# First stage of a hybrid decoder layer: q, k, v of two neighbouring heads and one gate, in wider weight runs, with a new order of heads and groups

## The chip, the cores and the metric

The kernel runs on one core of a Trainium2 chip. A core has a matrix engine (TensorE, PE in the profile), three engines for element-wise work (VectorE or DVE, ScalarE or ACT, GpSimd or POOL), a queue engine (SyncE, SP) that issues most transfers, and 16 DMA engines that move data between HBM and the on-chip memory. The metric is device time in microseconds (us), lower is better.

## The reference

One inference step of one layer, for a prompt of 1024 tokens and for 8 sequences of one new token each, in float32 with width 2048. What matters here, shortened:

```python
def mixer_layer(x, c, ...):
    mod = silu(c) @ w_ada + b_ada                       # w_ada 2048 x 6144
    shift, scale, gate = split(mod, 3)
    h = rmsnorm(x, norm_g) * (1 + scale) + shift
    z = h @ w_in                                        # w_in 2048 x 8208
    b_a, c_a, h_a, g_a, qkv, g_b, beta_logit, alpha_logit = split(z)
    # A: 8 groups of 128 channels
    y_a = b_a * causal_conv3(c_a * h_a) * silu(g_a)
    # B: 8 heads of 128
    q, k, v = split(silu(causal_conv4(qkv)))
    q, k = l2norm(q), l2norm(k)
    o, s = gated_delta_rule(q, k, v, g, beta, s0)       # chunked, one state per head
    o = rmsnorm(o, o_norm_g) * silu(g_b)
    y = concatenate([y_a, o]) @ w_out                   # 2048 x 2048
    return x + gate * y, ...
```

A final RMSNorm follows. The convolution states and the delta-rule states are outputs too.

## The kernel before, in words

**Layout.** Activations are kept transposed, channels on the 128 partitions and tokens along the free axis. The tokens go in two halves: 512 prompt tokens first, then 512 prompt tokens with the 8 samples. In each half `w_in` is taken in columns of 128 channels, each the k, q, v or gate of one head (`h(i, part)`, parts 0 to 3) or the C, h, gate or B of one group (`a(i, part)`, where part 0 is the two columns C and h). A `product` of a column sums 16 tiles of 128 rows in a PSUM bank. For precision, weights and activations are split in a high and a low fp32r part, and three passes (`hh·whi`, `hl·whi`, `hh·wlo`) are summed, so a product in the first half is 48 matmuls of 512 tokens.

**Weights.** `Stream` loads weights in tiles `raw` of 256 KB through SP's queue (six buffers), in the order in which they will be used. For each, ScalarE makes `whi`, and GpSimd or VectorE makes `wlo` (three buffers of each). SP's queue works in order: a load that waits for a free `raw` buffer holds up what is issued behind it.

**First stage (the ramp).** The conditioning product `silu(c) @ w_ada` needs 64 tiles `wat` of 512 KB, in runs of 1 KB (steps of two row tiles) or 2 KB (steps of four). It goes in six steps (`steps`), each giving shift and scale for 2 or 4 row tiles of `h`: `matvec` sums on TensorE, `spread` evicts the sums, transposes them and makes `s1` and `sh`, and `make_h` makes the row tiles `hh` and `hl`. Beside it, products of seven columns are accumulated in seven PSUM banks `pss`, row tile by row tile as `h` comes (`first_products`): C, h and gate of group 2, and k, q, v and gate of head 2 (`FIRSTS = (2, 2)`). Six of these columns have "pair" tiles: two row tiles of two columns, loaded by two issues of 128 KB with runs of 512 B (`add_pair`). The seventh has tiles of its own (`RONE`). Dummy matmuls (`busy`, 214 at the most) run at the very start. While TensorE would wait for `wat` tiles, `fill` gives it products.

**After it.** The logits of the decay gates follow (`logits_part`, on tiles `wlt`), then the remaining columns in the order that `order(half)` writes out by hand, then the output projection. The heads' delta rule runs beside the products: `gdn_prep`, `gdn_invert` (a triangular solve on VectorE with round trips through memory: `ub`, `tb`, `xd`, `yc`, issued from ScalarE's queue) and `gdn_apply`, one `chain` per head in the order `HEADS` = 2, 1, 3, 4, 7, 5, 0, 6. `conv_silu` evicts a k, q or v bank to `zr` on ScalarE and then does the convolution on VectorE, a tanh on ScalarE and a product on VectorE.

**The planner.** All engines work in order, and the order of the instructions is made when the program is built: `_Order` keeps a clock for each engine, with estimated costs (in `_Tensor.mm` for matmuls, in `_transfer` for transfers). Side work is written as generators that yield what they wait for; between matmuls, `pump` runs those steps whose inputs are ready by these clocks. So a changed cost or order moves side steps to other places in the stream. The price of a matmul of the fp32r kind was

```python
            if rhs.dtype == F32R:
                cost = max(n / 2250.0, 0.05) + 0.004
```

whatever stands before it. Line 370 in the profile is the call in `mm`, line 321 that of the other engines' operations; both are helpers, so groups are told apart by tile names.

Of the kernel before, what the change touches and what calls it, by code (L numbers as in the profile page):

```python
# [16 lines left out]
P = 128  # L17
# [345 lines left out]
class _Tensor:  # L363


    def __init__(self, od, pe):
        self.od, self.pe = od, pe

    def mm(self, out, lhsT, rhs, cost=None, **kw):
        r = self.pe.matmul(out, lhsT, rhs, **kw)  # L370
        if cost is None:
            n = _size(rhs)
            if rhs.dtype == F32R:
                cost = max(n / 2250.0, 0.05) + 0.004
            elif kw.get("is_transpose"):
                cost = 0.109
            else:
                cost = max(4 * n / 2400.0, 0.21) + 0.006
        self.od.put("P", [lhsT, rhs], [out], cost)
        return r  # L380


def _trunk(ctx, tc, nc, xT, w_in, w_ada, w_out, pack, consts, vecs, csq, ssm, yT, cap, cqp, ssp, cas, cqs, sss):
# [18 lines left out]
    def mm_tile():  # L402
        return ps_mm.tile([P, 512], F32, tag="mm", name="mm")
# [169 lines left out]
    class Stream:  # L573
# [9 lines left out]
                src = w[kq * 512:(kq + 1) * 512, col:col + P].rearrange("(k p) n -> p k n", p=P)  # L583
                self.todo.append(((col, kq), [(0, 4, src)]))

        def add_pair(self, w, cols, kp):

            self.todo.append(((cols, kp), [
                (2 * i, 2 * i + 2, w[kp * 256:(kp + 1) * 256, c:c + P].rearrange("(k p) n -> p k n", p=P))
                for i, c in enumerate(cols)]))  # L590

        def landed(self):

# [9 lines left out]
        def ahead(self, most=SPL):  # L603

            while True:
                if self.loaded < min(self.split + (4 if self.eager else RAW), len(self.todo)):
                    raw = wp.tile([P, 4, P], F32, tag="raw", name="raw", bufs=RAW)
                    for a, b, src in self.todo[self.loaded][1]:
                        SY.dma_start(raw[:, a:b, :], src)
                    self.raws.append(raw)  # L610
                    self.loaded += 1
                elif most and self.split < min(self.freed + SPL, self.loaded) and (
                        self.eager or self.split < self.used + 2 or self.landed()):
                    whi = wp.tile([P, 4, P], F32R, tag="whi", name="whi", bufs=SPL)
                    wlo = wp.tile([P, 4, P], F32R, tag="wlo", name="wlo", bufs=SPL)
                    split_w(self.raws[self.split], whi, wlo)
                    self.raws[self.split] = None
                    self.done.append((whi, wlo))
                    self.split += 1
                    most -= 1  # L620
                else:
                    return
# [151 lines left out]
        yield  # L774
        return th

    def conv_silu(half, t, pss, blocks, out, ready, zr=None):

        own = zr is None
        if own:  # L780
            hold("zr", 2)
            zr = tp.tile([P, WH + 3], F32, tag="zr", name="zr")
        for ps, (a, b) in zip(pss, blocks):
            S.activation(zr[:, 3 + a:3 + b], ps[:, :b - a], AF.Copy)
        if half == 0:
            G.memset(zr[:, 0:3], 0.0)
        else:
            G.tensor_copy(zr[:, 0:3], halo[:, t, :])

        def rest():  # L790
            yield [zr[:]]
            if half:
                G.tensor_copy(zs[:, t, :], zr[:, 3 + HT:3 + WH])
            G.tensor_copy(halo[:, t, :], zr[:, HT:HT + 3])
            w = [pkv("wq", t * 4 + j, 1) for j in range(4)]
            V.tensor_scalar(out, zr[:, 0:HT], w[0], None, ALU.mult)
            for j in range(1, 4):
                V.scalar_tensor_tensor(out, zr[:, j:j + HT], w[j], out, ALU.mult, ALU.add)
            if own:
                held["zr"] -= 1  # L800
            yield
            th = yield from tanh_half(out, HT)
            V.scalar_tensor_tensor(out, th[:, :HT], 1.0, out, ALU.add, ALU.mult)
            held["tm"] -= 1
            ready.append(out)
        od.spawn(rest())
# [450 lines left out]
    nca = cp.tile([P, 8, 2, NS], F32, name="nca")  # L1257
    sta = pkv("sa").rearrange("p (g j b) -> p g j b", j=2, b=NS)

    def group_a(half, g, blocks, y, pch=None):  # L1260
        n = WH if half else HT
        pc = pch[0] if pch else product(w_in, 1024 + g * P, range(4), hs, blocks)
        hold("ca", 1)
        c_ = tp.tile([P, WH], F32, tag="ca", name="c_", bufs=1)
        for ps, (a, b) in zip(pc, blocks):
            S.activation(c_[:, a:b], ps[:, :b - a], AF.Copy)
        phh = pch[1] if pch else product(w_in, 2048 + g * P, range(4), hs, blocks)
        hold("zr", 2)
        u = tp.tile([P, WH + 3], F32, tag="zr", name="ua")
        for ps, (a, b) in zip(phh, blocks):  # L1270
# [22 lines left out]
            held["zr"] -= 1  # L1293
        od.spawn(conv())
        yield
        pg = pch[2] if pch else product(w_in, 3072 + g * P, range(4), hs, blocks)
        hold("ca", 1)
        gc = tp.tile([P, WH], F32, tag="ca", name="gc", bufs=1)
        for ps, (a, b) in zip(pg, blocks):
# [17 lines left out]
            V.tensor_tensor(y[:, a:b], y[:, a:b], ps[:, :b - a], ALU.mult)  # L1317
        yield

    def head_tile(half, h, part, t, blocks, pss=None, zr=None):  # L1320

        if part < 3:
            c0 = 4096 + (1, 0, 2)[part] * 1024 + h * P
        else:
            c0 = 7168 + h * P
        if pss is None:
            pss = product(w_in, c0, range(4), hs, blocks)
        if part < 3:
            out = t["v"][:, :HT] if part == 2 else t["kq"][:, part, :]
            conv_silu(half, (1, 0, 2)[part] * 8 + h, pss, blocks, out, t["ready"], zr)  # L1330
            return
        n = WH if half else HT
        gb = t["gb"]
        for ps, (a, b) in zip(pss, blocks):
            S.activation(gb[:, a:b], ps[:, :b - a], AF.Copy)

        def silu():
            yield [gb[:]]
            th = yield from tanh_half(gb[:, :n], n)
            V.scalar_tensor_tensor(gb[:, :n], th[:, :n], 1.0, gb[:, :n], ALU.add, ALU.mult)  # L1340
            held["tm"] -= 1
            t["ready"].append(gb)
            if half:
                yield
                G.tensor_copy(gbs[:, h, :], t["gb"][:, HT:WH])
                sampled.append(h)
        od.spawn(silu())
# [7 lines left out]
    def order(half):  # L1355


        def h(i, *parts):
            return [("h", i, part) for part in parts or range(4)]

        def a(i, *parts):
            return [("a", i, part) for part in parts]
        if half == 0:
            r = a(2, 2) + h(1) + a(1, 0) + h(3) + a(1, 1) + h(4) + a(1, 2) + h(7, 0) + a(3, 0) + h(7, 1) + a(3, 1)
            r += h(7, 2) + a(3, 2) + h(7, 3) + h(5) + a(4, 0) + h(0, 0) + a(4, 1) + h(0, 1) + a(5, 0) + h(0, 2) + h(6)
            r += a(4, 2) + h(0, 3) + a(0, 0) + a(5, 1, 2) + a(0, 1) + a(6, 0) + a(0, 2)
            return r + a(6, 1) + a(7, 0) + a(6, 2) + a(7, 1, 2)
        r = h(2) + a(2, 0) + h(1) + a(0, 0) + h(3) + a(0, 1) + a(2, 1, 2) + a(0, 2) + a(1, 0) + h(4)
        r += h(7, 0) + a(1, 1, 2) + h(7, 1) + a(3, 0) + h(7, 2) + h(5) + h(7, 3) + a(3, 1, 2)
        r += h(0, 0) + a(4, 0) + h(0, 1) + a(4, 1, 2) + h(0, 2) + h(6) + h(0, 3)  # L1370
        return r + a(5, 0, 1, 2) + a(7, 0) + a(6, 0) + a(7, 1) + a(6, 1, 2) + a(7, 2)

    FIRSTS = (2, 2)
    HEADS = [i for kind, i, part in order(1) if (kind, part) == ("h", 0)]
    LASTG = order(1)[-1][1]

    HCOLS, ACOLS = (5120, 4096, 6144, 7168), (1024, 2048, 3072, 0)
    ADA = 9

    ra, rh = (tuple(c + i * P for c in cols) for cols, i in zip((ACOLS, HCOLS), FIRSTS))  # L1380
    RCOLS, RONE = (ra[:2], rh[:2], rh[2:]), ra[2]
    for kp in range(NK // 2):
        for c in RCOLS:
            ws.add_pair(w_in, c, kp)
# [51 lines left out]
    with ExitStack() as pools:  # L1436
# [17 lines left out]
        def first_products(f, nf):  # L1454

            for i in range(3):
# [2 lines left out]
                whi, wlo = rw[i]  # L1459
                for j in range(2):  # L1460
                    for k in range(f, f + nf):
                        jj = 2 * j + k % 2
                        passes(pss[2 * i + j], whi[:, jj, :], wlo[:, jj, :], *hs[k], 0, HT, k == 0, k == NK - 1)
                        yield
                if i == 2 and (f + nf) % 4 == 0:
# [81 lines left out]
        for step, (f, nf) in enumerate(steps):  # L1547
# [11 lines left out]
            for _ in spreading:  # L1559
                pass  # L1560
            if step == 0:
                pss = [mm_tile(), mm_tile(), mm_tile(), tp_tile(), ch_tile(), o_tile(), ch_tile()]
            for k in range(f, f + nf):
                if k % 4 == 0:
                    hs += h_quad()
# [9 lines left out]
                pass  # L1575
        S.activation(wl[:, :, 0:16], lr, AF.Copy)
        V.tensor_tensor(wl[:, :, 16:32], lr, wl[:, :, 0:16].bitcast(F32), ALU.subtract)
        ramp = [[p] for p in pss]
        od.rings = 1.0
        od.spawn(ws.run())  # L1580

# [83 lines left out]
    for half in range(2):  # L1665
# [3 lines left out]
        with ExitStack() as pools:  # L1669
# [6 lines left out]

            def chain(h, half, queue, done, gp):

                while len(queue) <= h or len(queue[h]["ready"]) < 2 or recd[half] < h - 1:
                    yield 0.2  # L1680
                t = queue[h]
                yield [t["kq"][:], MARGIN]
                cx = yield from gdn_prep(half, HEADS[h], gp, t)
                yield from gdn_invert(half, h, gp, t["kq"], cx)
                yield from gdn_apply(half, h, HEADS[h], gp, done, cx, t["kq"], t["gb"])

# [8 lines left out]
            def head(i, parts, pss=None):  # L1695
                for part in parts:
# [8 lines left out]
                    if part == 2:  # L1705
                        t["v"] = od.pin(yp.tile([P, WH], F32, tag="y", name="v"))
                    zr = yp.tile([P, WH], F32, tag="y", name="zr0") if pss and part < 3 else None
                    head_tile(half, i, part, t, blocks, [pss[part]] if pss else None, zr)

            groups = {}  # L1710
            if half == 0:
                g0 = FIRSTS[0]
                ys[g0] = new_y()
                groups[g0] = group_a(0, g0, blocks, ys[g0], (ramp[0], ramp[1], ramp[6]))
                next(groups[g0])
                next(groups[g0])
                head(FIRSTS[1], range(4), [r[0] for r in ramp[2:6]])
                od.spawn(conditions())
            pl = [mm_tile() for _ in blocks]
            for k in range(NK):  # L1720
# [210 lines left out]
```

## Time and profile before

| | us |
|---|---|
| median of 3 runs | 2144.99 (2144.23 to 2147.16) |
| profiled execution, its own time | 2149.42 |
| its span, first to last instruction | 2147.6 |
| TensorE busy in the span | 2108.6 (98%) |
| VectorE busy | 1252.4 (58%) |
| ScalarE busy | 832.6 (39%) |
| GpSimd busy | 849.0 (40%) |

Two rows of the page show the first stage: it cuts the span in 40 slices of 53.7 us, and gives the busy share of the DMA engines in tenths and what they moved. In the first two slices the DMA engines are at nine tenths, with 317 and 331 GB/s; from the fourth on they are mostly at half. The granted clock of TensorE is 0.993 over the span.

### The profile page before, as it was taken

The numbers are of one execution on the slowest core, as the hardware profiler recorded it, in microseconds if no ns is written. First come the engines' busy times: TensorE is split into PE (matmuls) and PEld (weight loads), VectorE is DVE, ScalarE is ACT, GpSimd is POOL, SyncE is SP. The second block draws the span as 40 slices with busy tenths as digits, with TensorE's granted clock in tenths as the row PEclk, the third lists the DMA queues.
The fourth block names the chain that finished last, engine by engine and source line by source line (L and its number), as shares of the span: only waits on it lengthen the run. The fifth ranks groups of instructions, "written<-read, shape, count | busy, mean of one in ns | idle before, by whom it ended". The sixth has DMA issues, their size and how long they took to land.

```text
span 2147.6 us, 40476 instructions
## 1 busy us (share of the span) xinstructions
PE 2108.6 (98%) x15045; PEld 1851.5 (86%) x15045; DVE 1252.4 (58%) x3635; ACT 832.6 (39%) x1885; POOL 849.0 (40%) x819
## 2 busy tenths in 40 slices
PE   8999999999999999999999999999999999999997
PEld 6468777777887887878889999999999999999997
DVE  3346776756867745287124767646576486435544
ACT  3234333434443333343233334243443333335554
POOL 1223333434344444423434343444443433445544
PEclk8999999999999999999999999999999999999998
DMA  9974765897454456955444564568664446968766
GB/s 317 331 231 83 159 147 145 137 159 135 113 114 96 88 106 84 82 180 181 142 104 105 125 120 108 121 107 110 112 91 91 90 100 100 91 92 239 228 210 203
DMA packets 466598, 299.66 MB, mean 140 GB/s; under 512 B 37600, under 2 KB 429536, under 8 KB 466400
## 3 DMA queue, kind: packets, MB, share of 16 engines
q1 hardware_dynamic: 442608, 284.26, 61.7%
q10 hardware_dynamic: 23792, 12.81, 2.5%
q8 instruction: 118, 1.93, 0.4%
q14 instruction: 80, 0.66, 0.1%
HBM read 277.06 MB, written 19.94 MB: 138 GB/s over the span
## 4 chain that ended last, share of the span: by engine, by line
PE 52%; DVE 2%; DMA 1%; POOL 0%; issue 0%; ACT 0%; POOLq 0%; ACTq 0%; DVEq 0%
PE mm L370 48%; PE cht L370 2%; PE tpt L370 1%; DVE xb L321 1%; PE ot L370 1%; DVE ob L321 0%; DMA tb<-ub 0%; DVE kq L321 0%; POOL wlo L321 0%; DMA ub<-dU 0%; POOL res L321 0%; DVE sl L321 0%; DVE y L321 0%; DVE wlo L321 0%; DMA xr<-in_xT 0%
## 5 line engine op out<-in xcount | busy, mean ns | idle before, releaser
L321 POOL TENSOR_TENSOR wlo<-raw,whi 128x512 fp32r<-128x512 f32 x547 | 731.4, 1338 | 1204.6 <-ACT whi L321 1026.9
L370 PE MATMUL mm<-hh,whi 128*128 128x264 f32 (+1 forms) x3008 | 969.2, 322 | 5.4 <-ACT hh L321 1.9
L370 PE MATMUL mm<-hl,whi 128*128 128x264 f32 (+1 forms) x3008 | 968.1, 322 | 5.2 <-DVE hl L321 5.0
L370 PE MATMUL mm<-hh,wlo 128*128 128x264 f32 (+1 forms) x3008 | 968.7, 322 | 0.6 <-POOL wlo L321 0.6
L321 ACT ACTIVATE whi<-raw 128x512 fp32r<-128x512 f32 x672 | 421.2, 629 | 686.3 <-PE mm L370 473.5
L370 PEld LDWEIGHTS mm<-hh,whi 128*128 128x128 f32 x3008 | 566.9, 188 | 54.0 <-issue 7.7
L370 PEld LDWEIGHTS mm<-hl,whi 128*128 128x128 f32 x3008 | 567.0, 188 | 50.0 <-DVE hl L321 7.4
L370 PEld LDWEIGHTS mm<-hh,wlo 128*128 128x128 f32 x3008 | 567.0, 188 | 41.4 <-issue 1.7
L370 PE MATMUL mm<-yhi,wlo 128*128 128x512 f32 (+2 forms) x768 | 246.1, 320 | 3.9 <-POOL wlo L321 3.2
L370 PE MATMUL mm<-ylo,whi 128*128 128x512 f32 (+2 forms) x768 | 246.3, 321 | 0.0
L370 PE MATMUL mm<-yhi,whi 128*128 128x512 f32 (+2 forms) x768 | 245.7, 320 | 0.0
L321 DVE TENSOR_TENSOR ob<-tb,xb 128x62 f32<-128x62 f32 (+30 forms) x992 | 200.7, 242 | 3.6 <-DMA tb<-ub 3.6
L321 DVE TENSOR_TENSOR xb<-xb,ob 128x62 f32<-128x62 f32 (+30 forms) x992 | 202.6, 244 | 0.0
L370 PEld LDWEIGHTS mm<-yhi,wlo 128*128 128x128 f32 x768 | 144.5, 188 | 16.6 <-POOL wlo L321 3.9
L370 PEld LDWEIGHTS mm<-ylo,whi 128*128 128x128 f32 x768 | 144.4, 188 | 12.4 <-issue 1.2
L370 PEld LDWEIGHTS mm<-yhi,whi 128*128 128x128 f32 x768 | 144.5, 188 | 11.6 <-ACT whi L321 0.3
L321 DVE TENSOR_TENSOR wlo<-raw,whi 128x512 fp32r<-128x512 f32 x125 | 89.2, 715 | 58.8 <-ACT whi L321 58.3
L321 DVE SCALAR_TENSOR_TENSOR kq<-zr,pk,kq 128x512 f32<-128x512 f32 x96 | 102.4, 1066 | 3.4
L321 DVE SCALAR_TENSOR_TENSOR res<-mm,ga,xr 128x512 f32<-128x512 f32 (+2 forms) x48 | 27.3, 568 | 118.5 <-PE mm L370 109.0
L321 DVE TENSOR_TENSOR acc<-acc,sqt 128x512 f32<-128x512 f32 (+3 forms) x70 | 56.8, 816 | 32.0 <-ACT sqt L321 31.2
L321 DVE SCALAR_TENSOR_TENSOR rt<-cht,gt_neg,v 128x128 f32<-128x128 f32 x56 | 19.5, 348 | 72.9 <-PE cht L370 72.9
L321 ACT ACTIVATE u<-cht,sm 128x128 f32<-128x128 f32 x64 | 23.5, 368 | 89.1 <-DVE u L321 87.6
(410 smaller groups left out, 1988.6 us busy)
## 6 DMA issues: line engine op xcount, KB each, us to landing
raw<-in_w_in SPq DMA_DIRECT2D x488, 256.0 KB, 5.2
raw<-in_w_out SPq DMA_DIRECT2D x160, 256.0 KB, 3.2
wat<-in_w_ada SPq DMA_DIRECT2D x64, 512.0 KB, 7.7
gw<-in_w_ada SPq DMA_DIRECT2D x64, 256.0 KB, 7.2
tb<-ub ACTq DMA_DIRECT2D x16, 512.0 KB, 6.5
raw<-in_w_in SPq DMA_DIRECT2D x48, 128.0 KB, 6.0
sl<-in_ssm SPq DMA_DIRECT2D x12, 512.0 KB, 6.4
x1s<-in_xT SPq DMA_DIRECT2D x16, 260.0 KB, 5.4
```

What stands on the lines that cost most here:

```text
L321: r = f(*args, **kw)
L370: r = self.pe.matmul(out, lhsT, rhs, **kw)
```

## The change

- The seven columns of the ramp are now k, q, v and gate of head 2 and k, q, v of head 1 (`FIRSTS = (2, 1)`). Heads 1 and 2 are neighbours in `w_in`, so a pair tile is two row tiles of 256 adjacent columns: one issue of 256 KB with runs of 1 KB. The gate of head 2 keeps tiles of its own.
- The banks are given out in another order, and a `busy` call spends what is left of the dummies before.
- Both heads are evicted after the ramp, head 2 first; head 1's convolution steps start later by 8, 12 and 16 us of the planner's clock (`LATER`).
- The order of the remaining columns of the first half is new. That of the second half is as before.
- A head's chain starts only when the preparation of the head before it is done.
- The planner charges 0.084 us more for an fp32r matmul that follows one of another kind.

```diff
     def mm(self, out, lhsT, rhs, cost=None, **kw):
...
+        if rhs.dtype == F32R:
+            cost += 0.084 if self.small else 0.0
+        self.small = rhs.dtype != F32R
...
-        def add_pair(self, w, cols, kp):
-            self.todo.append(((cols, kp), [
-                (2 * i, 2 * i + 2, w[kp * 256:(kp + 1) * 256, c:c + P].rearrange("(k p) n -> p k n", p=P))
-                for i, c in enumerate(cols)]))
+        def add_pair(self, w, col, kp):
+            src = w[kp * 256:(kp + 1) * 256, col:col + 2 * P].rearrange("(k p) n -> p k n", p=P)
+            self.todo.append(((col, kp), [(0, 4, src)]))
...
-                        SY.dma_start(raw[:, a:b, :], src)
+                        dst = raw[:, a:b, :]
+                        if src.shape[-1] > P:
+                            dst = dst.rearrange("p (k i) n -> p k (i n)", k=src.shape[1])
+                        SY.dma_start(dst, src)
...
-            yield [zr[:]]
+            yield [zr[:]] + [late] * (late > 0)
...
         if half == 0:
-            r = a(2, 2) + h(1) + a(1, 0) + h(3) + a(1, 1) + h(4) + a(1, 2) + h(7, 0) + a(3, 0) + h(7, 1) + a(3, 1)
-            r += h(7, 2) + a(3, 2) + h(7, 3) + h(5) + a(4, 0) + h(0, 0) + a(4, 1) + h(0, 1) + a(5, 0) + h(0, 2) + h(6)
-            r += a(4, 2) + h(0, 3) + a(0, 0) + a(5, 1, 2) + a(0, 1) + a(6, 0) + a(0, 2)
+            r = h(1, 3) + a(2, 0) + h(3, 0) + a(2, 1) + h(3, 1) + a(2, 2) + h(3, 2, 3) + a(1, 0) + a(1, 1) + a(4, 0)
+            r += h(4) + a(1, 2) + h(7, 0) + a(3, 0) + h(7, 1) + a(3, 1) + h(7, 2) + a(3, 2) + h(7, 3) + h(5) + h(0, 0)
+            r += a(4, 1) + h(0, 1) + a(5, 0) + h(0, 2) + h(6)
+            r += a(4, 2) + h(0, 3) + a(5, 1) + a(0, 0) + a(6, 0) + a(0, 1) + a(5, 2) + a(0, 2)
             return r + a(6, 1) + a(7, 0) + a(6, 2) + a(7, 1, 2)
...
-    FIRSTS = (2, 2)
+    LATER = 4.0
+    FIRSTS = (2, 1)
...
-    ra, rh = (tuple(c + i * P for c in cols) for cols, i in zip((ACOLS, HCOLS), FIRSTS))
-    RCOLS, RONE = (ra[:2], rh[:2], rh[2:]), ra[2]
+    RCOLS, RONE = tuple(c + min(FIRSTS) * P for c in HCOLS[:3]), HCOLS[3] + FIRSTS[0] * P
...
-                        jj = 2 * j + k % 2
+                        jj = 2 * (k % 2) + j
...
             if step == 0:
-                pss = [mm_tile(), mm_tile(), mm_tile(), tp_tile(), ch_tile(), o_tile(), ch_tile()]
+                busy(spare[0])
+                pss = [tp_tile(), mm_tile(), ch_tile(), mm_tile(), o_tile(), mm_tile(), ch_tile()]
...
-                while len(queue) <= h or len(queue[h]["ready"]) < 2 or recd[half] < h - 1:
+                while len(queue) <= h or len(queue[h]["ready"]) < 2 or recd[half] < h - 1 or (
+                        h and "prepared" not in queue[h - 1]):
                     yield 0.2
...
                 cx = yield from gdn_prep(half, HEADS[h], gp, t)
+                t["prepared"] = True
...
+                    late = LATER * (part + 2) if pss and len(queue) > 1 else 0.0
...
             if half == 0:
-                g0 = FIRSTS[0]
-                ys[g0] = new_y()
-                groups[g0] = group_a(0, g0, blocks, ys[g0], (ramp[0], ramp[1], ramp[6]))
-                next(groups[g0])
-                next(groups[g0])
-                head(FIRSTS[1], range(4), [r[0] for r in ramp[2:6]])
+                head(FIRSTS[0], range(4), pss[1:6:2] + pss[6:])
+                head(FIRSTS[1], range(3), pss[0:6:2])
```

More of the change, by code (lines that the diff above doesn't have):

```diff
@@ L366, in __init__ @@
     def __init__(self, od, pe):
-        self.od, self.pe = od, pe
+        self.od, self.pe, self.small = od, pe, False
     def mm(self, out, lhsT, rhs, cost=None, **kw):
@@ L775, in tanh_half, with conv_silu @@
         return th
-    def conv_silu(half, t, pss, blocks, out, ready, zr=None):
+    def conv_silu(half, t, pss, blocks, out, ready, zr=None, late=0.0):
         own = zr is None
@@ L1258, in _trunk, with group_a @@
     sta = pkv("sa").rearrange("p (g j b) -> p g j b", j=2, b=NS)
-    def group_a(half, g, blocks, y, pch=None):
+    def group_a(half, g, blocks, y):
         n = WH if half else HT
-        pc = pch[0] if pch else product(w_in, 1024 + g * P, range(4), hs, blocks)
+        pc = product(w_in, 1024 + g * P, range(4), hs, blocks)
         hold("ca", 1)
@@ L1266, in group_a @@
             S.activation(c_[:, a:b], ps[:, :b - a], AF.Copy)
-        phh = pch[1] if pch else product(w_in, 2048 + g * P, range(4), hs, blocks)
+        phh = product(w_in, 2048 + g * P, range(4), hs, blocks)
         hold("zr", 2)
@@ L1295, in group_a @@
         yield
-        pg = pch[2] if pch else product(w_in, 3072 + g * P, range(4), hs, blocks)
+        pg = product(w_in, 3072 + g * P, range(4), hs, blocks)
         hold("ca", 1)
@@ L1318, in group_a, with head_tile @@
         yield
-    def head_tile(half, h, part, t, blocks, pss=None, zr=None):
+    def head_tile(half, h, part, t, blocks, pss=None, zr=None, late=0.0):
         if part < 3:
@@ L1329, in head_tile @@
             out = t["v"][:, :HT] if part == 2 else t["kq"][:, part, :]
-            conv_silu(half, (1, 0, 2)[part] * 8 + h, pss, blocks, out, t["ready"], zr)
+            conv_silu(half, (1, 0, 2)[part] * 8 + h, pss, blocks, out, t["ready"], zr, late)
             return
@@ L1577, in _trunk @@
         V.tensor_tensor(wl[:, :, 16:32], lr, wl[:, :, 0:16].bitcast(F32), ALU.subtract)
-        ramp = [[p] for p in pss]
         od.rings = 1.0
@@ L1707, in head @@
                     zr = yp.tile([P, WH], F32, tag="y", name="zr0") if pss and part < 3 else None
-                    head_tile(half, i, part, t, blocks, [pss[part]] if pss else None, zr)
+                    late = LATER * (part + 2) if pss and len(queue) > 1 else 0.0
+                    head_tile(half, i, part, t, blocks, [pss[part]] if pss else None, zr, late)
             groups = {}
             if half == 0:
-                g0 = FIRSTS[0]
-                ys[g0] = new_y()
-                groups[g0] = group_a(0, g0, blocks, ys[g0], (ramp[0], ramp[1], ramp[6]))
-                next(groups[g0])
-                next(groups[g0])
-                head(FIRSTS[1], range(4), [r[0] for r in ramp[2:6]])
+                head(FIRSTS[0], range(4), pss[1:6:2] + pss[6:])
+                head(FIRSTS[1], range(3), pss[0:6:2])
                 od.spawn(conditions())
```

## The prediction

> **What bounds the kernel now.** I read the page first, then the busy time by stretch, then the list of TensorE's waits in the ramp, then single rows of the timeline. First the page:
>
> ```profile
> span 2147.6 us, 40476 instructions
> PE 2108.6 (98%) x15045; PEld 1851.5 (86%) x15045; DVE 1252.4 (58%) x3635; ACT 832.6 (39%) x1885; POOL 849.0 (40%) x819
> ```
>
> TensorE is busy 98% of the span, so a change can gain only what lies in the other 39 us, or work that it removes from TensorE. Next the stretches (columns: stretch, length, busy time and instructions of PE, PEld, DVE, ACT, POOL, then granted clock, DMA share, GB/s):
>
> ```profile
> 41.00:50.00 9.00, 5.92 (x24) 3.48 (x27) 5.40 (x6) 2.10 (x4) 3.23 (x3) 0.64 1.09 351
> 50.00:60.00 10.00, 9.53 (x76) 5.84 (x72) 0.51 (x3) 1.23 (x2) 2.02 (x2) 0.98 0.93 285
> 60.00:90.00 30.00, 26.69 (x149) 13.30 (x142) 10.90 (x26) 7.46 (x11) 5.14 (x4) 1.00 1.01 347
> 90.00:120.00 30.00, 29.16 (x176) 15.92 (x178) 15.83 (x28) 9.66 (x15) 6.43 (x5) 1.00 0.99 319
> 120.00:166.00 46.00, 46.00 (x266) 33.62 (x259) 15.42 (x28) 12.92 (x21) 14.37 (x15) 1.00 0.67 187
> 166.00:950.00 784.00, 776.29 (x4143) 614.54 (x4142) 507.54 (x1559) 308.09 (x720) 307.06 (x295) 1.00 0.64 121
> 1115.00:2090.00 975.00, 969.23 (x8585) 958.11 (x8583) 585.13 (x1766) 398.08 (x956) 416.25 (x416) 1.00 0.63 123
> 2090.00:2147.60 57.60, 43.34 (x355) 42.22 (x355) 30.49 (x78) 23.73 (x45) 27.98 (x22) 0.90 0.70 209
> ```
>
> Two things are to be seen. Until 120 us the DMA share is about 1: the first stage keeps the DMA engines full. But from 50 us on TensorE is nearly full too: it lacks 0.47 us in the ten from 50, 3.31 from 60 to 90, 0.84 from 90 to 120, and nothing from 120 to 166. Both being full, faster transfers gain only TensorE's holes. The projection of the first half lacks 7.71 us (784.00 less 776.29), that of the second 5.77, and the tail 14.26. Which holes are in the ramp, after the first products:
>
> ```profile
> PE mm L370 <- DVE hl L321: 2.0, 3, 1.3
> PE tpt L370 <- DVE sm L321: 0.9, 2, 0.5
> PE tpt L370 <- ACT ev L321: 0.7, 1, 0.7
> PE mm L370 <- POOL wlo L321: 0.6, 1, 0.6
> PE mm L370 <- ACT whi L321: 0.2, 1, 0.2
> ...
> 40.77 0.49 PE L370 MATMUL mm<-hh,whi 128*128 128x512 f32 x1 [1.90 <-ACT hh L321]
> 45.32 0.80 PE L370 MATMUL mm<-hl,whi 128*128 128x512 f32 x1 [2.27 <-DVE hl L321]
> 58.28 0.39 PE L370 MATMUL ot<-hl,whi 128*128 128x512 f32 x1
> 58.51 0.40 PE L370 MATMUL ot<-hh,wlo 128*128 128x512 f32 x1
> 58.75 0.60 PE L370 MATMUL tpt<-cs,ev 128*128 128x128 f32 x4
> 59.81 0.64 PE L370 MATMUL tpt<-wat,sc 128*32 128x512 f32 x4 [0.47 <-DVE sm L321]
> 64.86 0.50 PE L370 MATMUL mm<-hl,whi 128*128 128x512 f32 x1 [1.34 <-DVE hl L321]
> 83.22 0.66 PE L370 MATMUL tpt<-cs,ev 128*128 128x128 f32 x4 [0.74 <-ACT ev L321]
> 165.87 0.40 PE L370 MATMUL mm<-hh,wlt 128*128 128x512 f32 x1
> ```
>
> (In rows of the timeline: start, duration, then the idle time before it and who ended it.) The waits from 50 to 125 us add up to 4.4 us. Those behind hl, sm and ev (3.6) stand where one step of the conditioning product gives way to the next: its sums are evicted, transposed and made into h, and TensorE has no products of the step before left to fill the time. At 58.51 the last product of rows 0 and 1 ends, at 58.75 the transposes follow, and the next h is there only at 64.86. The waits on wlo and whi (0.8) are for a weight tile that was split late.
>
> **The change part by part.** *Wider runs.* Six of the ramp's seven columns come as three pairs of neighbours. 24 tiles of 256 KB are loaded with 24 issues in place of 48, in runs of 1 KB in place of 512 B. What each width reaches is seen where one kind of transfer has the queues to itself: 86 to 90 us (2 KB runs of the conditioning weights), 20 to 28 us (1 KB runs of them), 30 to 32 us (the pair tiles), in this order:
>
> ```profile
> DMA packets 821, 1.59 MB, mean 396 GB/s; under 512 B 47, under 2 KB 47, under 8 KB 821
> DMA packets 3052, 2.76 MB, mean 345 GB/s; under 512 B 109, under 2 KB 3051, under 8 KB 3051
> DMA packets 698, 0.39 MB, mean 197 GB/s; under 512 B 37, under 2 KB 698, under 8 KB 698
> ...
> raw<-in_w_in SPq DMA_DIRECT2D x48, 128.0 KB, 6.0
> ...
> 21.70 8.09 SPq L321 DMA_DIRECT2D raw<-in_w_in  x8
> 29.83 11.15 SPq L321 DMA_DIRECT2D wat<-in_w_ada  x9
> ```
>
> 24 tiles of 0.262 MB are 6.29 MB: 31.9 us at 197 GB/s, 18.2 us at 345, so 13.7 us of transfer time go. Four of the 24 tiles stand ahead of the ninth conditioning tile on SP's queue (8 issues, 8.09 us), so that tile and all behind it come 4 × 0.57 = 2.3 us earlier by the transfers, up to 4 us by the issues. The transfers are not what ends the ramp, though: with TensorE full, the matvecs move forward in its stream and products move back. That is just what fills the holes. By the step change at 58.75 about 2.3 us, or three passes of three matmuls (0.23 us from 58.28 to 58.51), are left over for the stretch from 59.81 to 64.86, and more at 83. The late tile's 0.8 go with its earlier landing. I take all 4.4 us. The ends: 0, if the waits come from the planner's optimism about VectorE and ScalarE and not from a lack of products; 7.5, with the 3.08 us that TensorE lacks from 41 to 50 as well. I leave those out of the sum, because they hang on the first h and on VectorE, and the tiles for the first step were issued ahead of every weight. What is late next is the chain to h itself, hidden as long as products are left.
>
> By the Trainium skill ("DMA: Bandwidth & Descriptors", Specifications) 512 B is already enough for line rate, so the wider runs would save no transfer time and the sum would be 2145.0. The three rows disagree: 197 against 345 GB/s.
>
> *The rest of the ramp.* TensorE gets the same 336 product matmuls in another order of banks. The added call that spends what is left of the dummy matmuls finds none left: there are 214 of them, each shown as two instructions,
>
> ```profile
> L370 PE MATMUL cht<-ones 32*32 32x32 f32 x428 | 21.9, 228 | 1.0 <-POOL nhalf L321 1.0
> ```
>
> and all 428 lie in the ramp's start, so the cost is 0; were some left, they would fall into the 1.90 us hole before 40.77.
>
> *What is evicted when.* Before, seven banks hold group 2 (C, h, gate) and head 2; now head 2 (k, q, v, gate) and head 1 (k, q, v). ScalarE gets seven evictions in place of six and one on VectorE. Head 1's three convolutions come forward. The rows of one, and of what its queue did to ScalarE:
>
> ```profile
> 168.06 0.48 DVE L321 TENSOR_SCALAR kq<-zr,pk 128x512 f32<-128x512 f32 x1
> 168.57 2.33 DVE L321 SCALAR_TENSOR_TENSOR kq<-zr,pk,kq 128x512 f32<-128x512 f32 x3
> ...
> 177.05 0.64 ACT L321 ACTIVATE th<-kq 128x512 f32<-128x512 f32 x1 [7.39 <-DVE gc L321]
> 178.07 0.62 ACT L321 ACTIVATE whi<-raw 128x512 fp32r<-128x512 f32 x1
> ```
>
> Three at 0.48 + 2.33 are 8.4 us of VectorE there, in place of the group's own steps. Already before, ScalarE stood 7.39 us behind VectorE with the next weight split queued behind it (178.07), and TensorE did not wait, since it had the logits and split tiles. The added delays of 8, 12 and 16 us keep head 1's steps out of that queue, and head 2's k, q and v are now evicted ahead of the gate. Cost 0, under that cover; if it is gone, every further us on ScalarE there is a us on TensorE, at the most those 8.4.
>
> *Order, the new condition and the planner's price.* Every product of the first half is still made once. The new condition holds a head's preparation until that of the head before is done. Behind it queue only that head's own steps, and the heads have slack: the last one's first state is written at 864.3 us (first of the row's eight at 293.9), the first weight of the output projection is used at 943.50.
>
> ```profile
> L321 DVE COPY st<-cht x8: 278/288/293, 293.9 to 864.3; 128x128 f32<-128x128 f32 x8
> 943.50 0.51 PE L370 MATMUL mm<-yhi,wlo 128*128 128x512 f32 x1 [1.15 <-POOL wlo L321]
> ```
>
> The planner now charges 0.084 us where a product matmul follows a small one. No instruction comes of it, but every side step after the ramp may sit some matmuls elsewhere. So the holes after the ramp (7.71 and 5.77 us) are dealt anew. I take them as unchanged, 0, since nothing says which way; the ends are half of them, 6.7 us, either way. The tail keeps its order.
>
> **Sum.** 2147.6 − 4.4 = 2143.2 us of span. The profiled execution took 2149.42 us with 1.8 around its span, 4.4 above the median of the runs, so I subtract from the median: 2144.99 − 4.4 = 2140.6.
>
> **Rivals.** *Hidden anyway:* the holes are waits for VectorE and ScalarE, so the transfers' gain goes into earlier landing alone. For it: four of the five waits name DVE or ACT. Against it: they occur only where products ran out. Time 2145.0. The skill's rule above would end here too, by another road; the rates leave it little chance, and it is inside this one's.
>
> *More than the holes:* the whole 13.7 us of transfers come through, 2131.3. For it: the DMA share of 1 to 120 us. Against it: TensorE is full from 120 to 166 us, after the share has fallen to 0.67. It would also need the slow clock (0.64 from 41 to 50 us) or holes after the ramp to go; a part of it, 5 us beyond the forecast, is the likelier form.
>
> *Slower:* a head's solve waits in ScalarE's queue for a round trip through memory, and TensorE behind it. There is one such place before:
>
> ```profile
> ACT sp L321 <- DMA xd<-xb: 5.2, 1, 5.2
> 345.99 0.38 PE L370 MATMUL tpt<-sp 128*128 128x256 f32 x1 [2.62 <-ACT sp L321]
> 346.72 0.94 PE L370 MATMUL tpt<-sp 128*128 128x256 f32 x5 [0.34 <-DVE sp L321]
> ```
>
> ScalarE is held 5.2 us by the transfer behind which the read is queued, and TensorE loses 2.62 + 0.34 = 2.96. The sixteen heads pass this place once each. With the 0.084 us charged, the planner's clock runs faster per matmul, so it puts the read fewer matmuls behind the write. Two such stalls more than now cancel the gain (2 × 2.96 = 5.9 against 4.4), and from three on (8.9) it is slower beyond 0.2%: 2140.6 + 8.9 = 2149.5.
>
> **How the numbers follow.** A measurement of this kernel can tell about 0.2%, 4.3 us, from no change: 2140.7 and 2149.3 are the bounds. The forecast, ramp holes gone and the rest within some us, has 0.50 (its own range 2136 to 2145, half of it below 2140.7); more than the holes 0.15; hidden anyway 0.16; slower by new stalls 0.19, of which 0.02 stay under the bound. So faster 0.25 + 0.15, and 0.01 from redealt holes in the hidden case: 0.41; same 0.25 + 0.15 + 0.02 = 0.42; slower 0.17. The range: 2133 below, which leaves out the full 13.7 us, and 2150 above, the sum with three stalls and a little more.
>
> **What would show it.** Right: pair tiles in 24 issues of 256 KB; a rate near 345 GB/s while they run alone; no waits on hl, sm or ev from 55 to 90 us; the logits starting near 161.5 us (before: 165.87, the first row on wlt); the stretch after the ramp lacking some 7.7 us again. Wrong: the logits starting at 165 us or later with the waits still there, or more than 12 us lacking between the logits and the output projection, with sp or whi named.

## The result and the profile after

The changed kernel is slower: 2163.16 us in the median of 6 runs (2160.79 to 2165.12) against 2147.87 for the kernel before in the same comparison, a ratio of 1.0073 with a 95% interval of 1.0063 to 1.0083. That is 15.3 us; the forecast was 4.4 us less, the range ended at 2150. The first two lines of the page after:

```profile
span 2163.0 us, 40443 instructions
PE 2115.0 (98%) x15045; PEld 1852.0 (86%) x15045; DVE 1251.8 (58%) x3630; ACT 830.9 (38%) x1885; POOL 859.7 (40%) x824
```

TensorE has the same 15045 instructions, yet is busy 6.4 us longer and idle 9 us longer. To see where, the span is cut at marks that both kernels have: first product, first and last matmul of the logits, first and last of each output projection. Busy time by stretch (columns as in the prediction), the kernel before, then the one after; the four rows of each are the ramp, the first projection, the second, and the last output projection:

```profile
40.77:165.87 125.10, 117.40 (x668) 72.23 (x669) 48.18 (x88) 33.60 (x53) 31.19 (x28) 0.97 0.88 277
173.06:922.09 749.03, 742.47 (x3998) 587.68 (x3997) 476.89 (x1508) 293.39 (x695) 299.73 (x287) 1.00 0.65 119
1110.77:1937.04 826.27, 822.21 (x7291) 814.01 (x7289) 507.63 (x1600) 318.78 (x777) 339.95 (x357) 1.00 0.60 103
1937.04:2133.72 196.68, 192.66 (x1677) 189.13 (x1676) 104.84 (x236) 104.23 (x226) 101.40 (x76) 1.00 0.78 228
```

```profile
40.79:167.06 126.27, 119.51 (x668) 72.53 (x669) 47.14 (x89) 34.85 (x55) 33.26 (x33) 0.97 0.86 271
174.26:928.69 754.43, 743.23 (x3998) 586.48 (x3997) 470.37 (x1507) 292.31 (x694) 301.30 (x287) 1.00 0.64 118
1117.38:1950.96 833.58, 824.56 (x7291) 814.42 (x7289) 515.63 (x1599) 317.42 (x777) 344.55 (x358) 1.00 0.59 102
1950.96:2148.65 197.69, 194.09 (x1677) 190.16 (x1676) 103.77 (x234) 104.11 (x226) 101.63 (x78) 0.99 0.78 227
```

The ramp is 1.2 us longer, the first projection 5.4, the second 7.3, the last stage 1.0: 14.9 of the span's 15.4. The largest part lies in the second projection, whose columns and order the change does not touch. In it TensorE lacks 9.02 us in place of 4.06, and is busy 2.35 us more. Whom it waits for there, before and after:

```profile
PE mm L370 <- DVE y L321: 1.5, 1, 1.5
PE mm L370 <- ACT c__11661 L321: 0.8, 1, 0.8
PE mm L370 <- ACT c__16269 L321: 0.7, 1, 0.7
PE mm L370 <- DVE wlo L321: 0.7, 1, 0.7
PE tpt L370 <- DVE sp L321: 0.4, 1, 0.4
PE cht L370 <- DVE st L321: 0.3, 1, 0.3
PE mm L370 <- ACT zr L321: 0.3, 1, 0.3
```

```profile
PE tpt L370 <- DVE sp L321: 1.4, 3, 0.7
PE mm L370 <- ACT gc L321: 1.3, 1, 1.3
PE cht L370 <- DVE st L321: 1.1, 1, 1.1
PE mm L370 <- ACT y L321: 1.0, 1, 1.0
PE cht L370 <- ACT os__14020 L321: 0.9, 1, 0.9
PE mm L370 <- DVE y L321: 0.9, 1, 0.9
...
```

(Three groups more after, of 0.8 us and less.) There is no one big stall: the waits that are new or longer are around 1 us each, on VectorE and ScalarE, in the heads' steps (sp, st, os) and at evictions (gc, y).

### The profile page after: what moved, and what is told of

It is laid out like the page before. It is cut to its first block, busy times and chain, and to the rows that moved or that the text cites. A ratio compares the mean times of both kernels' runs of the same rounds, so it can differ in the third digit from the quotient of the medians.

```text
span 2163.0 us, 40443 instructions
## 1 busy us (share of the span) xinstructions
PE 2115.0 (98%) x15045; PEld 1852.0 (86%) x15045; DVE 1251.8 (58%) x3630; ACT 830.9 (38%) x1885; POOL 859.7 (40%) x824
## 4 chain that ended last, share of the span: by engine, by line
PE 49%; DVE 4%; DMA 1%; ACT 1%; issue 0%; POOL 0%; ACTq 0%; SPq 0%; POOLq 0%; DVEq 0%
PE mm L370 45%; PE cht L370 2%; PE tpt L370 1%; DVE ob L321 1%; DVE xb L321 1%; DMA xr<-in_xT 1%; DVE res L321 0%; PE ot L370 0%; DVE kq L321 0%; DVE wlo L321 0%; ACTq L321 0%; DMA tb<-ub 0%; ACT junk L321 0%; DVE y L321 0%; DMA raw<-in_w_in 0%
## 5 line engine op out<-in xcount | busy, mean ns | idle before, releaser
L321 POOL TENSOR_TENSOR wlo<-raw,whi 128x512 fp32r<-128x512 f32 x552 | 740.1, 1341 | 1205.2 <-ACT whi L321 1020.6
L321 DVE TENSOR_TENSOR ob<-tb,xb 128x62 f32<-128x62 f32 (+30 forms) x992 | 208.6, 250 | 5.6 <-DMA tb<-ub 5.6
L321 DVE TENSOR_TENSOR xb<-xb,ob 128x62 f32<-128x62 f32 (+30 forms) x992 | 190.8, 232 | 0.0
L321 DVE TENSOR_SCALAR u<-cht,sm 128x128 f32<-128x128 f32 x64 | 22.2, 347 | 62.0 <-PE cht L370 62.0
```

Source lines behind the costliest of these rows:

```text
L321: r = f(*args, **kw)
```

## The experiments

All comparisons are against the kernel before, on the same chip. Lengths of stages are taken from one profiled execution of each kernel, between the marks above.

**Which part of the change costs the time.** Two kernels take the planner's price out of the change, or add it alone to the kernel before:

```diff
  # e1: the changed kernel
-        if rhs.dtype == F32R:
-            cost += 0.084 if self.small else 0.0
  # e2: the kernel before
...
+        if rhs.dtype == F32R:
+            cost += 0.084 if self.small else 0.0
```

> The changed kernel without the planner's 0.084 us for an fp32r matmul after another kind; all else as changed. Theory P (the price places side steps too early for TensorE): the second projection goes back from 833.6 us to about 826, the first loses most of its 4.6 us of new holes, and the time lies within 4 us of the kernel before. Theory O (the first stage and the new order of the first half cost the time; the second half's holes are chance): no more than 4 us below the changed kernel, some 11 us above before.

> The kernel before with only the planner's 0.084 us added. Theory P: the second projection is some 7 us longer than before and the first some 4, so 8 to 15 us above before. Theory O: within 4 us of before.

Without the price the changed kernel took 2146.58 us, ratio 1.0002 (0.9991 to 1.0013). The price alone took 2164.06, ratio 1.0080 (1.0063 to 1.0096). So the price is the whole loss, and the first stage, the wider runs and the new order together are worth nothing that can be measured: the interval is 0.1% either way. The two projections of the kernel without the price, then those with the price alone:

```profile
168.61:920.10 751.49, 744.67 (x3999) 589.07 (x3997) 468.22 (x1507) 294.87 (x694) 299.68 (x287) 1.00 0.65 119
1108.05:1933.10 825.05, 822.03 (x7290) 814.01 (x7289) 507.83 (x1600) 319.24 (x777) 339.55 (x357) 1.00 0.59 103
```

```profile
171.60:929.11 757.51, 745.60 (x3999) 589.54 (x3998) 471.27 (x1503) 293.94 (x695) 302.59 (x291) 0.99 0.64 118
1117.98:1950.28 832.30, 824.57 (x7291) 814.46 (x7289) 516.21 (x1599) 317.62 (x777) 345.77 (x358) 1.00 0.59 103
```

The second projection goes back from 833.6 to 825.1 us, and with the price alone goes up to 832.3. In it, the kernel before and the one without the price have the same order of matmuls, and so have the changed kernel and the one with the price alone; the lengths within these pairs differ by 1.2 and 1.3 us, so less than that should not be read out of one execution.

**The delays and the wide runs.** In the changed kernel, the late starts of head 1 were taken away; and each pair tile was loaded by two issues of 512 B runs, at the planner's old times:

```diff
  # e4
-                    late = LATER * (part + 2) if pss and len(queue) > 1 else 0.0
+                    late = 0.0
  # e5
-                        SY.dma_start(dst, src)
+                        od.move("Y", src, dst, _transfer(src, dst) * od.rings)   # for pair tiles
+                        halves = raw[:].rearrange("p (k i) n -> p k i n", i=2)
+                        for i in range(2):
+                            nc.sync.dma_start(halves[:, :, i, :], src[:, :, i * P:(i + 1) * P])
```

> The changed kernel without the late starts of head 1's convolution steps (8, 12, 16 us of the planner's clock); the second half's stream of matmuls is the same as in the changed kernel. Theory D (VectorE's queue after the ramp is what the delays protect): ScalarE stands longer behind VectorE after the logits, and TensorE loses 1 to 5 us more between 174 and 250 us. Theory P: within 3 us of the changed kernel, since the second half has the same order and so the same holes, about 9 us of them.

> The changed kernel with each pair tile loaded by two issues in runs of 512 B; the planner's clock and every engine's order are those of the changed kernel. If the wider runs shorten the ramp: the logits start 2 to 5 us later than its 167.06, with waits on the conditioning tiles. If TensorE hides them: the same start within 1 us, and the same time.

Without the delays the kernel took 2166.1 us, ratio 1.0091 (1.0075 to 1.0108), which is not clear of the changed kernel's 1.0073. The profile decides for theory D there: ScalarE stands 13.4 us behind VectorE after the logits, against 5.1 with the delays, and TensorE waits 5.2 us for a split weight tile, where it did not wait at all in the changed kernel. The waits of ScalarE from 165 to 200 us, changed kernel first, and the row of TensorE without the delays:

```profile
ACT th L321 <- DVE y L321: 5.1, 1, 5.1
```

```profile
ACT th L321 <- DVE y L321: 13.4, 1, 13.4
...
180.47 0.79 PE L370 MATMUL mm<-hh,whi 128*128 128x512 f32 x1 [5.22 <-ACT whi L321]
```

With narrow runs it took 2162.63 us, ratio 1.0073 (1.0055 to 1.0092), no different from the wide ones. Its logits start at 169.16 us, 2.1 after those of the changed kernel, which the expectation gave as the sign that the wider runs shorten the ramp. Both have the same order of matmuls there, and TensorE waits 2.3 us for conditioning tiles in place of 0.8. In the whole time it does not show.

**How the price acts.** The first idea (S) was that the price takes away slack. Four kernels tested it:

```diff
  # e6, e7: the changed kernel
-            cost += 0.084 if self.small else 0.0
+            cost += 0.168 if self.small else 0.0       # e7: -0.084
  # e8: the changed kernel; e9: that without the price
-    SEM = {"P": 0.13, ...
+    SEM = {"P": 0.38, ...                              # e9: -0.12
```

> The changed kernel with the price doubled, 0.168 us. Theory S (the price takes away slack: the planner's clock runs faster per matmul, a step is placed fewer matmuls behind its inputs, and TensorE waits for them): 8 to 20 us above the changed kernel, with more idle time of TensorE in both projections (20 and 9 us were measured with the price, 10 without). Theory C (chance: each price deals the holes anew, and this one dealt badly): anywhere between the kernel before and the changed kernel, idle time not above 20 us.

> The changed kernel with a price of -0.084 us. Theory S: as fast as without the price or up to 6 us faster, idle time in both projections at or under 10 us. Theory C: a scatter to either side, with no reason to be under the kernel without the price.

> The changed kernel, price kept, with 0.25 us more in the planner's allowance between another engine's result and TensorE (SEM of P, 0.13 to 0.38): every step for TensorE sits about one 512-token matmul later. Theory S: most of the 16 us come back, 2145 to 2152, idle time in both projections back near 10 us. Theory C: no systematic gain, 2155 to 2170.

> The changed kernel without the price, and with 0.25 us less in the same allowance (0.13 to -0.12). Theory S: 8 to 25 us above the kernel without the price, with idle time in both projections as with the price or more. Theory C: within some 8 us of it to either side.

They took 2160.69, 2162.13, 2159.38 and 2159.25 us, ratios 1.0070 (1.0055 to 1.0085), 1.0084 (1.0062 to 1.0106), 1.0064 (1.0045 to 1.0083) and 1.0064 (1.0049 to 1.0079). Theory S in its plain form falls: doubling the price did not add, a negative price cost as much, and more allowance did not bring the time back. Only less allowance (e9) came out as S said. Chance (C) does badly too, though its 2155 to 2170 for e8 came true: it would hardly put five different shifts all near 1.007. So a new theory (R): the order before is a selected one, and any new deal costs. That was tested with prices too small to matter:

```diff
  # e10, e11, e12: the kernel before; e13: the changed kernel
...
+            cost += 0.010 if self.small else 0.0       # e11: -0.010, e12: 0.040, e13: 0.010
```

> The kernel before with a price of 0.010 us, an eighth of the change's. It makes no difference to what the planner knows, but deals the order anew from the first projection on. Theory R (the order of before is a selected one; any new deal of it costs, whatever its sign or size): 8 to 18 us above before, 4 to 9 of it in the second projection (826 us before). Theory Q (dose: the price costs in proportion to its size): within 4 us of before, second projection 825 to 828.

> The kernel before with a price of -0.010 us. Theory R: 8 to 18 us above before, as with +0.010. Theory Q: within 4 us of before.

> The kernel before with a price of 0.040 us. Theory R: 8 to 18 us above before. Theory Q: some 8 us above before, half of what 0.084 costs, and more than twice what 0.010 costs.

> The changed kernel with a price of 0.010 in place of 0.084 us. Its second half has the same stream of matmuls as the kernel before with 0.010. Theory R: 6 to 18 us above before, a first projection of 750 to 761 us. Theory Q: as the changed kernel without the price, within 4 us of before.

All four are as fast as before: 2147.92, 2147.67, 2147.82 and 2147.14 us, ratios 0.9994 (0.9983 to 1.0005), 0.9999 (0.9990 to 1.0009), 1.0003 (0.9993 to 1.0012) and 0.9994 (0.9982 to 1.0006). Theory R falls as well: a new deal alone costs nothing. (The deal is new: the traces of the kernel before and of e10 have the matmuls of both projections in different orders.) Its rival, a cost in proportion, fits 0.010 but not 0.040, which should have cost 8 us. So it takes a shift of the plan of a certain size, and somewhere between 0.040 and 0.084 it begins to cost.

Then what is shifted? The price makes TensorE slower in the plan against the other three engines. Four kernels shift that balance:

```diff
  # e14: the changed kernel x 1.022; e17: the same x 1.08
  # e15: that without the price x 0.96; e16: the same x 1.05
+        cost *= 1.022                                  # VectorE, ScalarE, GpSimd
         od.put(self.key, ins, out, cost, port)
```

> The changed kernel, price kept, with the planner's costs of VectorE, ScalarE and GpSimd raised by 2.2%, about what the price adds to TensorE's (some 190 switches of 0.084 us in some 720 to 800 us of each projection). Theory B (balance: the price alone makes TensorE slower in the plan against the other engines, so TensorE meets them late): most of the 16 us come back, at or under 2152. Theory H (the hand-written order fits the plan near the old costs, and any larger shift of costs, either way, costs time): 2155 or more.

> The changed kernel without the price, the planner's costs of VectorE, ScalarE and GpSimd lowered by 4%. Theory B: as with the price or worse, 2157 or more. Theory H: 2155 or more too.

> The changed kernel without the price, the planner's costs of VectorE, ScalarE and GpSimd raised by 5%, so that TensorE meets them later. Theory B: not slower than without the price, 2138 to 2149, with less idle time of TensorE. Theory H: 2155 or more.

> The changed kernel, price kept, the planner's costs of the other three engines raised by 8%. Theory B: at or under 2152. Theory H: 2155 or more, the shift of costs being the largest here.

They took 2151.31, 2158.18, 2158.34 and 2155.97 us, ratios 1.0027 (1.0015 to 1.0039), 1.0060 (1.0044 to 1.0076), 1.0059 (1.0041 to 1.0077) and 1.0052 (1.0035 to 1.0070). With the price kept and the others raised by about as much, more than half of the loss is back (1.0073 to 1.0027): the balance counts, as B said, though this one run is all that speaks for B against H. But raised too far, with or without the price, it costs again, as H said. Neither holds alone. In e14 the first projection (754.4 us in the changed kernel) is short again, and the second (833.6), where the largest part of the loss lay, hardly is:

```profile
173.65:921.19 747.54, 743.51 (x3998) 586.64 (x3997) 473.53 (x1506) 293.30 (x694) 298.53 (x288) 1.00 0.65 119
1108.58:1940.28 831.70, 825.19 (x7290) 816.34 (x7289) 512.21 (x1598) 318.15 (x777) 342.62 (x360) 1.00 0.59 103
```

The projections, first and second, of e7 (price negative) and e16 (others raised), in which TensorE is faster in the plan against the others, and then of e15 (others lowered), in which it is slower, as with the price:

```profile
172.13:932.12 759.99, 745.78 (x3998) 589.70 (x3997) 472.09 (x1511) 293.83 (x694) 294.73 (x283) 0.99 0.65 117
1120.08:1944.76 824.68, 822.49 (x7291) 814.27 (x7290) 518.02 (x1598) 318.01 (x777) 343.45 (x359) 1.00 0.59 104
```

```profile
173.70:929.40 755.70, 743.91 (x3999) 589.43 (x3998) 473.85 (x1517) 293.74 (x694) 291.99 (x280) 0.99 0.64 118
1117.69:1942.99 825.30, 822.03 (x7291) 813.97 (x7289) 509.70 (x1610) 317.55 (x777) 326.52 (x348) 1.00 0.59 103
```

```profile
169.48:920.21 750.73, 745.47 (x3998) 588.82 (x3997) 471.14 (x1504) 293.09 (x694) 305.11 (x290) 1.00 0.65 119
1110.04:1944.24 834.20, 826.18 (x7290) 816.18 (x7289) 514.72 (x1595) 318.67 (x777) 347.80 (x362) 1.00 0.59 102
```

The two projections do not answer alike. The second is short (824.7, 825.3) where the plan has TensorE fast against the others, and long (834.2; 833.6 with the price, 835.5 with the double price) where it has it slow. That a step is then put into the stream before its input is ready, so that TensorE waits, is the likely reading and not shown: 0.25 us more allowance left it at 832.1 (e8), the balance of e14 at 831.7, and e19 below, without the price but with five weight buffers, has 836.5. The first projection follows no one direction: it is long with TensorE fast (760.0, 755.7) and long with the price (754.4, and 757.5 with it alone), but short in e14 and e8 (747.5, 749.2) and 750.7 in e15. Between, from a price of -0.010 to 0.040, both are short: 745.8 to 752.2 and 822.4 to 828.8 us in the six kernels there. A weaker form of chance, by which only a large shift deals badly, is not excluded; it would have to explain why no shift of the costs from 0.084 up, to either side, came out below 1.0027.

**The ramp.** Two kernels, from the changed one without the price, asked why its holes stayed:

```diff
  # e18
-                fill(t, 3 if nf == 1 else 5)
+                fill(t, 2 if nf == 2 else 3)
  # e19: pair tiles after the first are not loaded (and RAW 6 -> 5)
...
+                    if self.loaded and self.todo[self.loaded][1][0][2].shape[-1] > P:
+                        self.raws.append(self.same)
+                        self.loaded += 1
+                        continue
...
```

> The changed kernel without the price, with fewer products taken into the ramp between two groups of the conditioning matvec (at most 2 row-tile products where a step has two row tiles, 3 else, instead of 5 and 3 by its count), so that products are left at the step changes. If the holes at the step changes come from a lack of products and the transfers are far enough ahead: the waits on hl, sm and ev between 50 and 90 us shrink from about 3.6 us to under 1.5, and the ramp, from the first product to the logits, is 2 to 4 us shorter than its 124.6. If the conditioning transfers set the steps: new waits on the conditioning tiles of the same size, the ramp no shorter than 124 us. The order after the ramp is dealt anew, so the whole time may differ by some us either way.

> The changed kernel without the price; 23 of the 24 pair tiles are not loaded, their products use the first tile's weights again (the splits are still made), and the stream has five buffers. So the 18 us that the wide pair tiles take of the queues are gone from the ramp; only the ramp is read. If those transfers hold up the ramp: from the first product to the logits well under 124.6 us, 118 or less. If the ramp is TensorE's work and the chain to h: 122 to 126 us, with the waits at the step changes still there.

The first took 2150.45 us, ratio 1.0017 (1.0007 to 1.0027); its ramp, from the first product to the logits, is 127.65 us against 124.61. TensorE's waits from 45 to 165 us in it, and then the row of the ramp without pair loads:

```profile
PE tpt L370 <- DMA wat<-in_w_ada: 4.2, 5, 2.0
PE tpt L370 <- ACT ev L321: 0.7, 1, 0.7
PE tpt L370 <- DVE sm L321: 0.5, 1, 0.5
PE tpt L370 <- DVE hl L321: 0.2, 1, 0.2
```

```profile
37.14:155.01 117.87, 115.36 (x652) 71.34 (x653) 46.65 (x87) 34.74 (x55) 35.93 (x35) 0.97 0.77 248
```

With products kept back, the waits at the step changes shrink to 1.4 us, and waits of 4.2 us on conditioning tiles take their place. Without pair loads the ramp is 6.7 us shorter, 2.7 of it idle time, and after the first steps no wait at a step change is left. (16 of the conditioning product's matmuls also run before the mark there, so part of the 6.7 is work done earlier.) So the transfers do hold up the ramp. Keeping products back only moved the waits; having the tiles earlier closed them.

## Why the prediction was wrong

**The step that failed: the planner's price taken at 0.** It was the whole loss: 1.0080 with the price alone, 1.0002 without it. The prediction said that no instruction comes of it and that the holes after the ramp are dealt anew, with half of them, 6.7 us, as ends. Idle time of TensorE in the two projections went from 6.56 and 4.06 us to 11.20 and 9.02, and their lengths by 5.4 and 7.3 us: 12.7 us, nearly twice that bound. Two things were missed. The bound was taken from the holes that the profile shows, while a shift of the plan can make as many again, as well as 2.35 us of longer busy time in the second projection. And "nothing says which way" treated the price as a new deal of the steps, but a new deal is not what costs: tiny prices, which deal anew too, cost nothing. That the price acts as a systematic shift of TensorE against the others fits e14 in part and is not shown.

**The slower rival** had the right part of the change, the price moving TensorE's clock in the plan, but the wrong place and size. It looked for more stalls of 2.96 us on sp behind a round trip. The changed kernel has many waits of about 1 us on VectorE and ScalarE. Its time of 2149.5 was 4.5 us above the kernel before; 15.3 were measured. That the kernel came out slower is therefore no success of this rival's sum.

**The ramp: 4.4 us of holes were to go; they stayed.** TensorE's rows after, as far as they match those shown before:

```profile
59.31 1.93 PE L370 MATMUL tpt<-wat,sc 128*32 128x512 f32 x16 [0.47 <-DVE sm L321]
64.36 0.50 PE L370 MATMUL tpt<-hl,whi 128*128 128x512 f32 x1 [1.32 <-DVE hl L321]
83.07 0.66 PE L370 MATMUL tpt<-cs,ev 128*128 128x128 f32 x4 [0.74 <-ACT ev L321]
111.73 0.64 PE L370 MATMUL tpt<-wat,sc 128*32 128x256 f32 x8 [0.61 <-DMA wat<-in_w_ada]
```

The three holes at the step changes are there to within 0.02 us. Those on wlo and whi went, and 0.8 us on conditioning tiles came. Over the whole ramp TensorE's idle time did fall, from 7.70 to 6.76 us, but with the same 668 matmuls it is busy 2.11 us longer, and 1.9 of that lies in the 128 matmuls that are 512 wide on conditioning tiles (16.4 us before, 18.3 after). Why these take longer is not shown. Where the start was quick, the kernel before with -0.010 and the changed one without the price, the ramps are 124.64 and 124.61 us long: nothing came of the 4.4 us. The rate was predicted about right (345 forecast, 321 measured): from 29 to 31 us the changed kernel and the one with narrow runs moved

```profile
DMA packets 656, 0.64 MB, mean 321 GB/s; under 512 B 30, under 2 KB 656, under 8 KB 656
```

```profile
DMA packets 820, 0.39 MB, mean 197 GB/s; under 512 B 50, under 2 KB 820, under 8 KB 820
```

(The Trainium skill's 512 B for line rate, "DMA: Bandwidth & Descriptors", Specifications, disagrees with the trace here too.) Part of the time saved on the queues turned into waits of SP's queue, which issues everything in order. Its waits from 40 to 140 us before, then after:

```profile
SPq L321 <- PE tpt L370: 20.4, 18, 2.7
SPq L321 <- DMA wat<-in_w_ada: 10.2, 13, 1.1
SPq L321 <- DMA cs<-in_consts: 7.3, 1, 7.3
...
```

```profile
SPq L321 <- PE tpt L370: 31.9, 18, 6.3
SPq L321 <- DMA cs<-in_consts: 8.4, 1, 8.4
...
SPq L321 <- DMA wat<-in_w_ada: 2.1, 3, 1.1
...
```

The queue waits 11.5 us more for TensorE to free conditioning buffers and 8.1 less for conditioning tiles to land; all its waits grow from 41.8 to 51.1 us. A load of constants holds it in both kernels, for 7.3 and 8.4 us, and no run moved that load. The prediction counted transfers and not what each load waits for on its queue.

**Right:** the rate; the pair tiles in half the issues; that head 1's convolutions cost nothing under the delays, and that without them ScalarE's hold becomes TensorE's (5.2 us, within the bound of 8.4); that the new condition costs nothing, though only as part of the kernel without the price, at 1.0002.

**What stays open.** How the price turns into waits is not shown: why the second projection stayed long when the balance was put back, what lengthens the first, and why the loss begins only between 0.040 and 0.084 us. That the hand-written order and delays suit the plan's balance near the old costs fits the times of all runs, but no run changed the order with the balance kept off. None of the versions beats the kernel before: the lowest ratio, 0.9994, includes 1.

## What to carry to other kernels

A cost in a planner that fixes the order of in-order engines is part of the kernel: changed on one engine alone, it shifts every step of that engine against the others, and even a price meant as a correction can make the kernel slower. Do not book it at 0 because no instruction comes of it; try it by itself, and try moving the other engines' costs with it (here 2.2% brought back more than half, and 8% did not). Before a faster transfer is booked as a gain, look at what the issuing queue waits for: the time saved may only be waited out at the next buffer.

## What the runs showed of the hardware

The start of the ramp has two forms under the same instructions. Up to the first product, the kernel before and the one with -0.010 have one stream on TensorE; the granted clock from 30 to 40 us (the third number from the end) was 0.66 in the one and 0.96 in the other, and the first product came at 40.77 and 37.42 us:

```profile
30.00:40.00 10.00, 8.16 (x89) 4.34 (x86) 3.26 (x7) 1.69 (x4) 1.27 (x1) 0.66 1.03 322
```

```profile
30.00:40.00 10.00, 6.85 (x78) 3.11 (x75) 5.90 (x10) 4.16 (x7) 2.60 (x3) 0.96 1.01 314
```

All twenty kernels fall into these two forms: eleven have their first product at 36.8 to 38.0 us with a granted clock of 0.90 to 0.97 from 30 to 40 us, nine at 40.6 to 40.9 with 0.53 to 0.70. In the kernel before the clock fell to 0.50 from 31 to 34 us although TensorE was busy all the time from 25 to 34, with short dummy matmuls and the conditioning product; with -0.010 it was 1.00 there. So being busy in the profile was not enough to keep the clock up there. The difference of 3.4 us is most of the 5 over which the kernel before spreads (2144.23 to 2149.25); that the two forms make that spread is likely and not shown, since one execution of it was profiled. By the Trainium skill ("TensorE: Matmul & The Clock Gate", What's actually happening) the clock follows TensorE's activity in windows of about 3.4 us that run freely of the kernel, so that one kernel can differ from run to run. The traces agree in kind, one stream having come out in two forms; that the place of the window decides is not shown by them.
